# Order of the up and down units in a Strassen-Winograd MLP, and its sums by copies and adding DMAs

## The chip, the cores and the metric

The kernel runs on one core of one Trainium2 chip. A core has a matrix engine (TensorE, PE in the profile) that multiplies from SBUF into the accumulator memory PSUM, a vector engine (VectorE, DVE), an activation engine (ScalarE, ACT), GpSimd (POOL) and SyncE (SP), which here only issues DMAs. Each engine works through its own queue in order; semaphores make one wait for another. The metric is the device time of one execution in microseconds (us), lower is better. Three runs of the kernel before gave 1293.41 to 1295.04 us, median 1294.1 us.

## What is computed

A decoder trunk of two layers on one sequence of 512 tokens with 1024 channels, in float32. Cut to what matters here:

```python
for i in range(2):
    hn = rmsnorm(h, norm_mix_g[i])
    h = h + (even_mixer if i % 2 == 0 else odd_mixer)(hn, ...)
    hn = rmsnorm(h, norm_mlp_g[i])
    u = jnp.square(jax.nn.relu(hn @ w_mlp_up[i]))        # 1024 -> 4096
    h = h + u @ w_mlp_down[i]                            # 4096 -> 1024
    gate = jax.nn.sigmoid(rmsnorm(h, norm_ple_g[i]) @ w_ple_gate[i])
    h = h + (p[i] @ w_ple_proj[i]) * gate
return rmsnorm(h, final_norm_g)
```

The change concerns the squared-ReLU MLP, the two lines with `u`.

## The kernel before

Activations lie transposed: the eight tiles `h[0]` to `h[7]` hold 128 channels each by 512 tokens. To keep float32 accuracy, every operand is split into a high part (rounded to fp32r) and a low part (the rest), and each product is three matmuls, high by high, high by low, low by high (`mm3`, L140; the three matmuls are lines 141, 144 and 145). ACT makes a high part by a copy, DVE the low part by a subtraction.

**The MLP in quarters.** The 4096 hidden channels are worked in four quarters, `ch` = 0 to 3. A quarter has four *up units* `up(ch, c)`: each loads 1 MB of weights (`wload`, two buffers `raw`), splits them (L122, L128), and computes two hidden tiles of 128x512 in 48 matmuls of 512 columns. DVE applies ReLU and the norm's factor (L757), ACT squares (L758). The two tiles of a unit are one *pair*, and four tokens-by-channels quadrants of it, and three sums of them (`T1`, `T2`, `T4`, lines 763 to 767), are the seven slices of the tile `u`. ACT and DVE split it into `uh` (L769) and `ul` (L770), which are 7x256 columns each.

A quarter also has four *down units* `down(ch, c)`, one for every two output tiles `h[2c]`, `h[2c+1]`. They use the Strassen-Winograd form: a 2x2 block product with seven products in place of eight. DVE makes the four weight sums `s13` and `s24` (lines 794, 795, 796, 799), and `split` makes the high and low parts of `w13`, `w24`, `w11` and `w` (L808, L809). `w13`, `w24` and `w` have the tags `wh`/`wl` with three buffers, `w11` the tag `e` with five. Each of the seven products runs over the quarter's four pairs: 4 x 3 = 12 matmuls of 256 columns. They go to four PSUM banks. Banks 2 and 3 belong to `h` and are added there (L877, L878). Banks 0 and 1 belong to sums that several blocks share; they are gathered over the quarters in `sides[c][0]` and `sides[c][1]` (`total`: ACT copies in quarter 0, L838; DVE adds in quarters 1 and 2, L840), and put into `h` once, by `side_sums` (L921).

**The order of units** is written out by hand at the end of `mlp`:

```python
for c in range(4):
    up(0, c)
for ch in range(1, NCH):
    up(ch, 0)
    for c in range(4):
        down(ch - 1, c)
    for c in range(1, 4):
        up(ch, c)
```

So a quarter's down units come after the first up unit of the next quarter, and the hidden tiles `uh` and `ul` have five buffers each. After quarter 3's up units there is no such unit to come between; there, the first down unit takes the pairs in two passes, `ks` = (0, 1, 2) and then (3,) (L858). In quarter 3 two more things differ. The sums `s13` come from DRAM by two copies on SP's queue and an adding DMA on POOL's (`add_up`, lines 778 and 779). And `total` goes through `collect`: an ACT copy to a staging tile (L833) and an adding DMA on POOL's queue (L834) into `sides`. The staging is the tile `u`, or for `c` = 1 a spare buffer of `ul` called `stage`; another spare buffer, of `uh`, holds `b12` for the last, plain down unit `down_last` (L895).

Within an engine, a scheduler at compile time chooses the order of instructions from priorities (the order in which they are written) and its estimate of times; `order(later, earlier)` adds an edge that forbids the other order. The kernel uses it at the first down unit of quarter 3 for the weight splits against the ReLU and the sums of `u`.

## Time and profile before

| | |
|---|---|
| median of 3 runs | 1294.1 us |
| profiled execution | 1294.54 us |
| its span, first to last instruction | 1292.8 us |
| granted TensorE clock | 0.998 |
| ACT busy | 708.3 us, 55% |
| DMA, mean rate | 112 GB/s |
| HBM read, written | 131.92 MB, 6.37 MB |

The page gives the busy time of each engine, a table of 40 slices, and the costliest groups of instructions with the idle time ahead of them. Besides the page there are views of the trace: who waited for whom, windows with the busy time of each engine, and the timeline, which lists instructions by start time (us from the span's start), duration, engine, line, operation, tiles written and read, and in brackets the idle time of that engine just before, with what ended it. A matmul's duration overlaps the next one's, so that the pace of PE is read from the starts.

### The profile page before, as it was taken

How to read it: one execution, taken by the hardware profiler on the slowest of the kernel's cores; microseconds unless marked ns; L12 is line 12 of the kernel's file. 1: busy time of each engine (PE TensorE's matmuls, PEld its weight loads, DVE VectorE, ACT ScalarE, POOL GpSimd, SP SyncE). 2: the span in 40 equal slices, each digit the busy share in tenths (PEclk: the TensorE clock that was granted, in tenths of full speed). 3: DMA queues.
4: the chain of work that ended last, by engine and by line, in shares of the span. 5: the costliest groups of instructions: out<-in, count | busy, mean ns of one | idle time of the engine just before them, and what ended most of it. 6: DMA issues, size and time to landing. Idle time of an engine off the chain costs nothing.

```text
span 1292.8 us, 19230 instructions
## 1 busy us (share of the span) xinstructions
PE 1273.7 (99%) x7488; PEld 1121.4 (87%) x7488; DVE 1003.9 (78%) x1665; ACT 708.3 (55%) x1146; POOL 214.1 (17%) x184
## 2 busy tenths in 40 slices
PE   9999999999999999999999999999999999999996
PEld 7988887888988989989889888788899898898986
DVE  7788898688848869678767777887785885986976
ACT  5767868555535344356456666765553443534544
POOL 2343433500000000001024333222000000000201
PEclk9999999999999999999999999999999999999999
DMA  6421523222232322648332222212223223254751
GB/s 209 146 82 50 163 74 115 90 98 98 98 103 93 119 103 76 192 110 222 134 130 83 82 90 80 68 58 90 106 98 108 88 98 126 71 158 136 174 177 66
DMA packets 33995, 144.25 MB, mean 112 GB/s; under 512 B 3888, under 2 KB 4624, under 8 KB 21232
## 3 DMA queue, kind: packets, MB, share of 16 engines
q1 hardware_dynamic: 29680, 135.16, 30.7%
q0 software_dynamic: 4224, 7.87, 3.5%
q8 instruction: 59, 0.97, 0.3%
q14 instruction: 32, 0.26, 0.1%
HBM read 131.92 MB, written 6.37 MB: 107 GB/s over the span
## 4 chain that ended last, share of the span: by engine, by line
PE 81%; DVE 10%; ACT 5%; issue 2%; DMA 2%; SPq 0%; POOL 0%; DVEq 0%; ACTq 0%
PE mm L141 11%; PE mm L144 11%; PE mm L145 10%; PE sc L144 5%; PE sc L145 5%; PE sc L141 5%; PE pv L144 4%; PE pv L145 4%; PE pv L141 4%; PE tp L145 4%; PE tp L144 4%; PE tp L141 4%; PE pv L574 3%; PE tp L553 2%; PE tp L895 2%
## 5 line engine op out<-in xcount | busy, mean ns | idle before, releaser
L122 ACT ACTIVATE wh<-raw 128x1024 fp32r<-128x1024 f32 (+1 forms) x156 | 160.6, 1034 | 141.0 <-PE mm L144 52.9
L126 POOL TENSOR_TENSOR wl<-raw,wh 128x512 fp32r<-128x512 f32 (+1 forms) x132 | 179.7, 1383 | 299.1 <-ACT wh L122 295.4
L141 PE MATMUL mm<-hi,wh 128*128 128x512 f32 x472 | 186.3, 395 | 0.4 <-DVE tmp L490 0.4
L145 PE MATMUL mm<-hi,wl 128*128 128x512 f32 x472 | 184.7, 391 | 0.0
L144 PE MATMUL mm<-lo,wh 128*128 128x512 f32 x472 | 184.5, 391 | 0.0
L128 DVE TENSOR_TENSOR wl<-raw,wh 128x1024 fp32r<-128x1024 f32 x90 | 109.6, 1223 | 38.2 <-ACT wh L122 34.1
L145 PEld LDWEIGHTS mm<-hi,wl 128*128 128x128 f32 x472 | 88.6, 188 | 19.9 <-POOL wl L126 0.4
L141 PEld LDWEIGHTS mm<-hi,wh 128*128 128x128 f32 x472 | 88.7, 188 | 17.2 <-DVE tmp L490 0.8
L144 PEld LDWEIGHTS mm<-lo,wh 128*128 128x128 f32 x472 | 88.7, 188 | 15.6
L779 POOL DMA_DIRECT2D s<-in_w_down_dram x4 | 4.5, 1122 | 581.6 <-DMA s<-in_w_down_dram 315.8
L808 ACT ACTIVATE wh<-s 128x1024 fp32r<-128x1024 f32 x58 | 61.1, 1053 | 54.8 <-DVE s L795 14.7
L547 ACT ACTIVATE e<-e,mn 128x128 f32<-128x128 f32 (+3 forms) x96 | 53.8, 561 | 62.2 <-DVE mn L544 61.8
L770 DVE TENSOR_TENSOR ul<-u,uh 128x1792 fp32r<-128x1792 f32 x32 | 64.8, 2024 | 29.5 <-ACT uh L769 29.4
L809 DVE TENSOR_TENSOR wl<-s,wh 128x1024 fp32r<-128x1024 f32 x58 | 70.9, 1222 | 16.9 <-ACT wh L808 16.6
L769 ACT ACTIVATE uh<-u 128x1792 fp32r<-128x1792 f32 x32 | 54.5, 1702 | 45.7 <-DVE u L767 45.7
L758 ACT ACTIVATE u<-u 128x512 f32<-128x512 f32 x64 | 39.7, 626 | 68.1 <-DVE u L757 67.9
L141 PE MATMUL sc<-hi,wh 128*128 128x512 f32 x184 | 72.3, 393 | 0.4 <-ACT hi L187 0.4
L144 PE MATMUL sc<-lo,wh 128*128 128x512 f32 x184 | 72.1, 392 | 0.4 <-DVE lo L188 0.3
L145 PE MATMUL sc<-hi,wl 128*128 128x512 f32 x184 | 72.0, 391 | 0.0
L141 PE MATMUL mm<-wh,hi 128*128 128x256 f32 (+1 forms) x216 | 63.1, 292 | 0.0
L145 PE MATMUL mm<-wh,lo 128*128 128x256 f32 (+1 forms) x216 | 63.0, 292 | 0.0
L144 PE MATMUL mm<-wl,hi 128*128 128x256 f32 (+1 forms) x216 | 62.8, 291 | 0.0
(304 smaller groups left out, 3874.3 us busy)
## 6 DMA issues: line engine op xcount, KB each, us to landing
raw<-in_w_up_dram SPq DMA_DIRECT2D x32, 1024.0 KB, 4.9
raw<-in_w_down_dram SPq DMA_DIRECT2D x32, 1024.0 KB, 4.9
raw<-in_w_in_dram SPq DMA_DIRECT2D x23, 1024.0 KB, 4.9
raw<-in_w_gate_dram SPq DMA_DIRECT2D x8, 1024.0 KB, 4.9
bias<-urow SPq DMA_DIRECT2D x24, 256.0 KB, 3.9
raw<-in_w_outa_dram SPq DMA_DIRECT2D x8, 768.0 KB, 4.1
pj<-pjd SPq DMA_DIRECT2D x16, 256.0 KB, 4.9
h<-in_xT_dram SPq DMA_DIRECT2D x8, 256.0 KB, 6.5
```

Source lines behind the costliest of these rows:

```text
L122: act = nc.scalar.activation(hi, src, AF.Copy)
L126: nc.gpsimd.tensor_tensor(lo[:, kx], src[:, kx], hi[:, kx].bitcast(F32), op=ALU.subtract)
L128: last_low[:] = [nc.vector.tensor_tensor(lo, src, hi.bitcast(F32), op=ALU.subtract).ins]
L141: mm = nc.tensor.matmul(acc, lh, rh, start=start, stop=False)
L144: nc.tensor.matmul(acc, lh, rl, start=False, stop=False)
L145: return mm.ins, nc.tensor.matmul(acc, ll, rh, start=False, stop=stop).ins
L547: nc.scalar.activation(e[:, 0:n], e[:, 0:n], AF.Exp, scale=-1.0, bias=mn, accum_out=s)
L758: chain.append(nc.scalar.activation(ui, ui, AF.Square, scale=0.5).ins)
L769: nc.scalar.activation(uh, u, AF.Copy)
L770: part = nc.vector.tensor_tensor(ul, u, uh.bitcast(F32), op=ALU.subtract)
L808: high[:] = [nc.scalar.activation(hi, src, AF.Copy).ins]
L809: low[:] = [nc.vector.tensor_tensor(lo, src, hi.bitcast(F32), op=ALU.subtract).ins]
```

## The change

The matmuls stay as many as they were. The diff does five things.

- **Order.** In every quarter all four up units come first, then its four down units. The first down unit of each quarter, not of the last alone, takes the pairs in two passes, and the edges that `order` adds there hold in each quarter.
- **Buffers.** `uh` and `ul` have four buffers in place of five. `b12` has tiles of its own for each `c`, and `stage` is a tile of its own, written only as `s13` of `down(3, 1)`.
- **Side sums.** `total` in quarters 1 and 2 goes through `collect` as in quarter 3: an ACT copy, then an adding DMA on POOL's queue. In quarter 0 the ACT copies stay.
- **State sums.** In quarters 0 to 2 the additions to `h` go through `collect` too (with the sign -1 for the second). In quarter 3 they stay on DVE.
- **Staging.** `collect` takes its staging from the tag `e` (five buffers).

Besides, the zeroing of the left part of `diag` (the second operand of the scan at L619) goes from DVE at the start to POOL, behind the first mixer's other memsets.

```diff
-    nc.vector.memset(diag[:, 0:S - P], 0.0)
...
+        if keep:
+            nc.gpsimd.memset(diag[:, 0:S - P], 0.0)
...
+            uh, ul = (fpool.tile([P, 7, HW], F32R, tag=t, name=nm(t), bufs=4) for t in ("uh", "ul"))
             u = fpool.tile([P, 7, HW], F32, tag="u", name=nm("u"), bufs=1)
             if ch == NCH - 1:
-                if c == 0:
-                    b12.append([fpool.tile([P, HW], F32R, tag=t, name=nm(t), bufs=1) for t in ("b12h", "b12l")])
-                else:
-                    if c == 1:
-                        spare.append(fpool.tile([P, 7, HW], F32R, tag="uh", name=nm("spare"), bufs=5))
-                        stages.append(fpool.tile([P, 7 * HW], F32, tag="ul", name=nm("stage"), bufs=5))
-                        add_up(stages[0][:, 0:2 * S].rearrange("p (s c) -> p s c", s=2), w_down[layer, 4 * ch + 1])
-                    b12.append((spare[0][:, 2 * c - 2], spare[0][:, 2 * c - 1]))
-            uh = fpool.tile([P, 7, HW], F32R, tag="uh", name=nm("uh"), bufs=5)
-            ul = fpool.tile([P, 7, HW], F32R, tag="ul", name=nm("ul"), bufs=5)
+                b12.append([fpool.tile([P, HW], F32R, tag=f"{t}{c}", name=nm(t), bufs=1) for t in ("b12h", "b12l")])
+                if c == 1:
+                    stages.append(fpool.tile([P, 2, S], F32, tag="stage", name=nm("stage"), bufs=1))
+                    add_up(stages[0], w_down[layer, 4 * ch + 1])
...
-            if last and c:
+            if c and (last or c == 1):
                 order(sum2, hidden[ch, 3][2] if c == 1 else lows[-1])
...
-            if last:
-                stage = [stages[0] if c == 1 else fpool.tile([P, 7 * HW], F32, tag="u", name=nm("u"), bufs=1), 0]
-
             def collect(dst, src, sign=1.0):
-                t = stage[0][:, stage[1]:stage[1] + src.shape[-1]]
-                stage[1] += src.shape[-1]
+                t = t2k("e")[:, 0:src.shape[-1]]
                 nc.scalar.activation(t, src, AF.Copy, scale=sign)
                 nc.gpsimd.dma_start(dst, t, accum_op=ALU.add)
...
-                elif not last:
-                    nc.vector.tensor_tensor(sides[c][x], sides[c][x], banks[bank], op=ALU.add)
                 else:
                     collect(sides[c][x], banks[bank])
...
-            if last and c == 0:
+            if c == 0:
                 order(low[0], hidden[ch, 3][3])
             lows.append(low[0])
             w11 = split(rv[:, A11:A11 + 1])
-            if last and c == 1:
+            if c == 1:
                 order(low[0], low13)
-            if last and c == 0:
+            if c == 0:
                 lows.clear()
...
-            for ks in ((0, 1, 2), (3,)) if last and c == 0 else (range(4),):
+            for ks in ((0, 1, 2), (3,)) if c == 0 else (range(4),):
...
-                    if last and c == 0:
+                    if c == 0:
                         order(high[0], hidden[ch, 3][4])
                         order(low[0], hidden[ch, 3][5])
...
-            nc.vector.tensor_tensor(h[2 * c], h[2 * c], banks[2], op=ALU.add)
-            nc.vector.tensor_tensor(h[2 * c + 1][:, 0:HW], h[2 * c + 1][:, 0:HW], banks[3][:, 0:HW], op=ALU.subtract)
+            if last:
+                nc.vector.tensor_tensor(h[2 * c], h[2 * c], banks[2], op=ALU.add)
+                nc.vector.tensor_tensor(h[2 * c + 1][:, 0:HW], h[2 * c + 1][:, 0:HW], banks[3][:, 0:HW], op=ALU.subtract)
+            else:
+                collect(h[2 * c], banks[2])
+                collect(h[2 * c + 1][:, 0:HW], banks[3][:, 0:HW], -1.0)
...
+        for ch in range(NCH - 1):
+            for c in range(4):
+                up(ch, c)
+            for c in range(4):
+                down(ch, c)
         for c in range(4):
-            up(0, c)
-        for ch in range(1, NCH):
-            up(ch, 0)
-            for c in range(4):
-                down(ch - 1, c)
-            for c in range(1, 4):
-                up(ch, c)
+            up(NCH - 1, c)
         side_sums(3)
```

More of the change, by code (lines that the diff above doesn't have):

```diff
@@ L733, in mlp @@
         sides = [[fpool.tile([P, S], F32, tag=f"side{x}{c}", name=nm("side"), bufs=1) for x in range(2)] for c in range(4)]
-        hidden, spare, stages, b12, low, lows, high = {}, [], [], [], [], [], []
+        hidden, stages, b12, low, lows, high = {}, [], [], [], [], []
         def up(ch, c):
@@ L786, in down @@
             if last and c == 1:
-                s13 = stages[0][:, 0:2 * S].rearrange("p (s c) -> p s c", s=2)
+                s13 = stages[0]
             else:
```

## The prediction, made before the changed kernel had run

> **What bounds the kernel now.** I read the page's head first, then the list of what the tensor engine waits for, then a table of windows around the stretches that the change reorders, and last the timeline of three engines at one seam.
>
> ```profile
> span 1292.8 us, 19230 instructions
> PE 1273.7 (99%) x7488; PEld 1121.4 (87%) x7488; DVE 1003.9 (78%) x1665; ACT 708.3 (55%) x1146; POOL 214.1 (17%) x184
> ```
>
> TensorE (PE) is busy for all but 1292.8 - 1273.7 = 19.1 us. The change alters the order of its matmuls, not their number: 7 products, 4 pairs and 3 matmuls a down unit before and after. So a gain can only come out of these 19.1 us, or out of matmuls that are issued late without showing as idle. How much of that lies in the MLP stage (274 to 610 us, and the same again in the second layer)?
>
> ```profile
> PE sc L145 <- DVE wl L809: 1.1, 1, 1.1
> PE mm L144 <- DVE ul L770: 0.9, 2, 0.4
> ```
>
> Of the twelve kinds of wait that PE shows, these two are the MLP's. Three waits, 2.0 us in all. The table of windows says where (columns after the window: length, then busy time and count of PE, weight loads, DVE, ACT, POOL, then clock, DMA share and rate):
>
> ```profile
> 409.70:449.70 40.00, 40.00 (x338) 40.00 (x337) 32.98 (x43) 15.93 (x16) 0.00 (x0) 1.00 0.30 106
> 565.90:598.30 32.40, 30.84 (x254) 30.14 (x253) 28.81 (x46) 19.76 (x26) 6.76 (x8) 1.00 0.64 158
> 1191.50:1222.70 31.20, 30.72 (x254) 30.21 (x254) 27.72 (x44) 19.76 (x26) 6.11 (x7) 1.00 0.67 163
> ```
>
> The first row is the down part of the second quarter: PE has no idle time at all, although DVE is at 33.0 of 40.0 us. 4 x 84 = 336 matmuls in 40.0 us are 0.119 us each. The other two rows are the down units of the last quarter in the two layers. Only there does a down unit follow its own fourth up unit directly, and only there does PE wait. That is exactly the seam which the change makes at three more places in each layer. So the kernel before holds two samples of its price.
>
> **The seam, second layer.**
>
> ```profile
> 1191.55 0.28 PE L141 MATMUL mm<-uh,wh 128*128 128x256 f32 x1
> ...
> 1199.21 0.28 PE L141 MATMUL mm<-uh,wh 128*128 128x256 f32 x1
> 1199.93 0.39 PE L144 MATMUL mm<-ul,wh 128*128 128x256 f32 x1 [0.44 <-DVE ul L770]
> ...
> 1202.76 0.28 PE L144 MATMUL tp<-ul,wh 128*128 128x256 f32 x1
> 1203.07 0.39 PE L145 MATMUL tp<-uh,wl 128*128 128x256 f32 x1
> ```
>
> The first down unit begins at 1191.55. Its first pass takes pairs 0 to 2: 63 x 0.119 = 7.5 us. The second pass, pair 3, needs the fourth unit's `ul`. Its second matmul starts 0.72 us after the first where 0.12 is the pace: **0.60 us** lost. At 1203.07, in the next unit's first product, the low half of its weights is late: 0.31 - 0.12 = **0.19 us**. (Gaps under 0.06 us are left out of the price; the first quarter has some too, without such a seam.) Together 0.79 us.
>
> ```profile
> 571.47 0.28 PE L144 MATMUL sc<-ul,wh 128*128 128x256 f32 x1
> 572.83 0.38 PE L145 MATMUL sc<-uh,wl 128*128 128x256 f32 x1 [1.08 <-DVE wl L809]
> ...
> 574.83 0.28 PE L141 MATMUL mm<-uh,wh 128*128 128x256 f32 x1
> 575.55 0.39 PE L144 MATMUL mm<-ul,wh 128*128 128x256 f32 x1 [0.44 <-DVE ul L770]
> ```
>
> In the first layer the same 0.60 us, and 1.36 - 0.12 = **1.24 us** before it, for the weights of the last two products. The cause lies some 16 us earlier, in DVE's queue:
>
> ```profile
> 549.89 0.69 DVE L796 TENSOR_TENSOR s<-s,raw 128x512 f32<-128x512 f32 x1 [2.90 <-issue]
> 1174.28 0.69 DVE L796 TENSOR_TENSOR s<-s,raw 128x512 f32<-128x512 f32 x1 [1.59 <-DMA raw<-in_w_down_dram]
> ```
>
> The weight sum of the coming down unit stands in DVE's queue and holds everything behind it until its weights have landed: 2.90 us in one layer, 1.59 in the other. The difference, 1.31 us, is about the 1.24 that PE pays. In both cases the landing shared the DMA engines with the copies and sums from DRAM that only the last quarter makes.
>
> **The change part by part.**
>
> *Order of units.* Removed: the one up unit (10.9 us of PE) that lay between the fourth up unit and the down units of quarters 0 to 2. Added: two passes in the first down unit, as in the last quarter. What covered the chain from accumulator to `ul` is now the 7.5 us pass. Six new seams. I start from 0.79 us each and correct by rows:
>
> ```profile
> 1192.68 0.43 DVE L762 TENSOR_TENSOR spare<-u,spare 128x256 fp32r<-128x256 f32 x1
> 1193.02 0.68 DVE L757 SCALAR_TENSOR_TENSOR u<-pv,rstd 128x512 f32<-128x512 f32 x1
> ...
> 1197.85 2.03 DVE L770 TENSOR_TENSOR ul<-u,uh 128x1792 fp32r<-128x1792 f32 x1 [0.69 <-ACT uh L769]
> ...
> 1201.79 1.23 DVE L809 TENSOR_TENSOR wl<-stage,wh 128x1024 fp32r<-128x1024 f32 x1 [0.59 <-ACT wh L808]
> 1202.93 0.68 DVE L877 TENSOR_TENSOR h<-h,sc 128x512 f32<-128x512 f32 x1
> ...
> 1203.86 1.22 DVE L809 TENSOR_TENSOR wl<-s,wh 128x1024 fp32r<-128x1024 f32 x1
> ```
>
> - L762 is made in the last quarter only. In the chain it stands ahead of the second L757, 1193.02 - 1192.68 = **-0.34 us**.
> - Against that, quarters 0 to 2 make two more weight sums a unit on DVE (L794, L795, 0.69 us each), but without the landing delay of 1.59 to 2.90 us, since no copies from DRAM run beside it. These two nearly cancel in the second layer's sample. I take 0; bounds -0.26 (what is then left of the 0.60) and +1.24 (the first layer's lateness).
> - The order of products differs: in quarters 0 to 2 the first unit's `w13` is read by the first and the third product of a pass, in the last by the first and second. Its buffer, which the next unit's `w13` needs, is free one product later, 3 x 0.119 = **+0.36 us**. The 0.19 grows by that.
>
> ```profile
> 1200.70 1.06 ACT L808 ACTIVATE wh<-stage 128x1024 fp32r<-128x1024 f32 x1 [2.88 <-PE mm L144]
> 1201.66 1.07 ACT L833 ACTIVATE u<-mm 128x512 f32<-128x512 f32 x2
> 1202.62 1.06 ACT L808 ACTIVATE wh<-s 128x1024 fp32r<-128x1024 f32 x1
> ```
>
> - The next unit's `w24` is now wanted by its second product, not its third. Counted on the second layer's clock: unit start 1202.40, plus 0.55 (0.19 + 0.36), plus 12 x 0.119 for one product and 0.24 to the third matmul = 1204.62. Its low half: ACT 1202.62 to 1203.68, and without L877 ahead of it DVE to about 1204.97: **+0.35 us**. On ACT two copies went ahead of that split; with the h copies four would. Bounds: 0 (split first) and +1.3 (two more copies of 0.4 to 0.6 us ahead).
>
> So 0.79 - 0.34 + 0.36 + 0.35 = 1.16 us for a seam.
>
> *Sums by copies and adding DMAs.* Per down unit of quarters 1 and 2 DVE loses two side adds (L840) and two h adds (L877, L878); quarter 0 loses the h adds only. PE had no idle time there, so DVE's relief is worth **0**. ACT gains copies of about 0.55 us (L833 above); in the 40 us window ACT had 15.9 busy, so 16 x 0.55 = 8.8 more has room. The adding DMAs are issued on POOL, idle there (0.00 in the window). The staging is the `e` tag with its 5 buffers, and these the units' `w11` halves use too:
>
> ```profile
> L834 POOL DMA_DIRECT2D side<-u x8: 878/1201/1552, 578.2 to 1220.5; - x8
> DMA to landing us min/median/max: 3.3/4.9/6.0
> 428.33 0.62 ACT L808 ACTIVATE e<-raw 128x512 fp32r<-128x512 f32 x1
> 434.67 0.69 DVE L809 TENSOR_TENSOR e<-raw,e 128x512 fp32r<-128x512 f32 x1
> ```
>
> The two `w11` halves made at 428.33 and 434.67 are those of the unit that starts at 439.7 and are read until its fourth product ends at 445.4: 17.1 + 10.7 = 27.8 buffer-us a unit. Four copies hold a buffer for 0.6 + 4.9 us each, 22.0. Together 49.8 of the 5 x 10.0 that there are. It just fits, since `w11` can be made later. At the seam of quarters 1 and 2 the next unit's `w11` low half may have to wait until the first side copy has landed: copy by about 2 us into the second pass, landed at 7 to 8, DVE 0.69, wanted at 2.5 + 4.3 + 0.24 plus the seam's own 0.5 = 7.5. Bounds 0 and 1.2; I take **+0.2 us** for four of the six seams.
>
> By the Trainium skill, "SBUF — State Buffer", section "SBUF: two separate sides", a DMA issued by GpSimd can starve, since its descriptors are written through a port pair that some VectorE instructions lock. The rows agree in kind: the issue (L834) took 878 to 1552 ns. Its text has 620 ns alone against 3100 beside such an operation; as an estimate by that page, 2.5 us more for each of the adds. The sum does without it, and what it would do is a rival below.
>
> *Fewer buffers for `uh`/`ul`* (4 for 5). The next quarter's first up unit can write `uh` only after the last down unit has read it, but it does so after its own 10.9 us of matmuls: **0**. If that cover went, the next seam would be late; it is four units away.
>
> *The last quarter.* `stage` and `b12` have buffers of their own, so the copies and the sum from DRAM for unit 1 no longer wait for a `ul` buffer, and can be out of the way of the landing at 549.89. That would give back the first layer's lateness: **-1.24 us**; bounds 0 and -2.6 (all that both last seams lose: 1.84 + 0.79).
>
> *The memset.*
>
> ```profile
> 0.89 0.38 DVE L194 MEMSET diag<- 128x384 f32 x1 [0.89 <-PEq L1147]
> 25.43 5.58 POOL L126 TENSOR_TENSOR wl<-raw,wh 128x512 fp32r<-128x512 f32 x4 [21.26 <-ACT wh L122]
> ```
>
> 0.38 us go from DVE, which waits for the first loads anyway; on POOL it falls into 21.26 us of idle time: **0**.
>
> **Sum.** Quarter 0: 2 x 1.16 = 2.3. Quarters 1 and 2: 4 x 1.36 = 5.4. Last seam -1.24. Together +6.5 us. The profiled execution took 1294.54 us (1.7 around its span), so 1301.0; it lies 0.44 above the median of the three runs, 1294.1, and against that I forecast **1300.6**.
>
> **Rivals.**
>
> 1. *The seams are covered.* The chain from the last accumulator to `ul` needs, with nothing between, about 0.69 + 0.63 + 0.69 + 2 x 0.42 + 1.71 + 2.03 = 6.6 us and some 0.5 of hand-overs: under the 7.5 of the pass. If DVE comes to the seam without lateness and the splits are placed between, the six seams cost 0 to 0.6 us each and the last gives up to 1.2 back: 1293 to 1296.5. For it: no landing delay. Against it: both samples show 0.60. Chance 0.25.
> 2. *Faster.* All six seams are covered and both last seams lose their waits too: 1294.1 - 2.6 = 1291.5, and a few small gaps more make 1291. It can hardly go lower, since the waits in the list end there. Chance 0.10.
> 3. *The `e` buffers throttle the units.* With a hold of 0.6 + 6.0 us (the slowest landing) the need is 27.8 + 26.4 = 54.2 of 50 buffer-us, a unit of 10.8 us instead of 10.0, and 16 units in quarters 1 and 2 of both layers lose 13 us beside the 6.5: about 1314. It decides from a landing above 4.95 us, and the rows have a median of 4.9. Against it: DVE and ACT can make `w11` later, and a bank is wanted again only two units on. The rule of the Trainium skill above would work here, and L834's 1552 ns agrees with it as far as it goes. Chance 0.15.
>
> **How the numbers follow.** The forecast, six seams partly exposed and +2.7 to +13 us in all, has 0.50. This kernel's measurement can tell about 0.2%, 2.6 us, from no change. Faster by more: 0.10 (rival 2). Within it: 0.25 (rival 1). Slower: 0.50 + 0.15 = 0.65. The range goes from 1291.8, which takes in nearly all of rival 1 and some of rival 2, to 1310, where six seams with the first layer's lateness end (6 x (1.16 + 1.24) + 0.8 = 15.2 on 1294.1) and below which part of rival 3 lies; about 0.2 is left out.
>
> **What would show it.** Right: in the profile after, the last matmul of each fourth up unit is followed 7.5 us later by a PE wait for `ul` L770, six new ones, and about 12 us after the seam by one for `wl` L809; the windows of the down parts grow from 40.0 to 41 or 42 us, those of the up parts stay at 43.5. DVE's busy time falls by about 49 us (of each layer, 8 units lose 2 x 0.69 + 0.69 + 0.42 and 4 lose 1.11) without effect. Wrong: no PE wait at the seams (rival 1); or waits spread over all units of quarters 1 and 2, with ACT or DVE waiting for adding DMAs (rival 3). A different count of matmuls, or another pace than 0.119 us, would overturn the whole argument.

## The result and the profile after

The changed kernel took **1302.38 us** (median of 4 runs, 1301.29 to 1302.88) against 1293.76 us (1293.3 to 1295.04) for the kernel before, run beside it: a ratio of 1.0066, with a 95% interval of 1.0055 to 1.0078. It is slower by about 8.6 us. The profiled execution's span is 8.2 us longer (1301.0 against 1292.8).

The head of the page, for the kernel after:

```profile
span 1301.0 us, 19540 instructions
PE 1277.3 (98%) x7488; PEld 1121.2 (86%) x7488; DVE 963.4 (74%) x1584; ACT 744.9 (57%) x1226; POOL 283.6 (22%) x265
```

The matmuls are as many as before, 7488. DVE lost 40.5 us of work and ACT gained 36.6; neither engine is the bottleneck, PE is still busy for 98% of the span. PE's idle time grew by 4.6 us (19.1 to 23.7), and its busy time by 3.6 with the same matmuls: part of a wait counts as busy, as the last section shows. The list of PE's waits, kernel after (total us, times, longest):

```profile
PE tp L145 <- DVE wl L805: 3.1, 6, 0.5
PE sc L145 <- DVE wl L805: 2.2, 2, 1.1
PE mm L144 <- DVE ul L766: 0.9, 2, 0.4
```

The first row is new: six waits, one for each new seam, all for the low half of a weight block. The second had one entry before and has two. The third is as before: the last quarter's two seams and no others.

The windows of the down parts, kernel after (length, busy time and count of PE, weight loads, DVE, ACT, POOL, then clock, DMA share, GB/s):

```profile
399.70:440.60 40.90, 40.37 (x337) 40.09 (x336) 26.61 (x30) 23.75 (x32) 12.04 (x14) 1.00 0.80 180
568.60:612.80 44.20, 42.51 (x326) 40.41 (x325) 39.82 (x64) 26.60 (x37) 8.91 (x10) 1.00 0.71 177
1197.90:1242.20 44.30, 42.50 (x326) 40.39 (x325) 39.51 (x64) 26.56 (x37) 8.87 (x10) 1.00 0.72 177
```

In the second quarter DVE's work fell from 33.0 to 26.6 us, ACT's rose from 15.9 to 23.8, POOL's from nothing to 12.0, and the DMA engines' share from 0.30 to 0.80. The part is 1.0 us longer (40.97 us in the table below, 40.00 before).

For all kernels below I measured each down part from the start of its first matmul to the start of the first matmul behind it (us; quarters 0, 1, 2 and the last, of layer 0 and then of layer 1):

| kernel | layer 0 | layer 1 | six seams | two last |
|---|---|---|---|---|
| before | 40.32, 40.00, 40.00; 43.69 | 40.32, 40.00, 39.99; 42.38 | 240.63 | 86.07 |
| after | 41.37, 40.97, 40.87; 44.17 | 41.39, 41.09, 40.97; 44.31 | +6.03 | +2.41 |
| e4, order alone | 41.93, 40.43, 40.42; 42.19 | 41.92, 40.44, 40.44; 41.99 | +4.95 | -1.89 |
| e5, sums alone | 40.32, 41.28, 40.78; 47.14 | 40.31, 40.46, 41.11; 46.31 | +3.63 | +7.38 |
| e12, side sums moved | 41.37, 40.86, 40.87; 41.57 | 41.38, 40.86, 40.87; 41.57 | +5.58 | -2.93 |
| e6, before with two edges | 40.31, 40.00, 40.00; 41.57 | 40.32, 40.00, 40.00; 41.57 | +0.00 | -2.93 |

The kernel after: 6.03 + 2.41 = 8.4 us, which accounts for the 8.2 by which its span grew. Each row is one profiled execution, and that of the kernel after is the longest of its four. In the profiles of e1 and e10, whose medians agree with the change, the two last parts are together 1.3 and 2.2 us shorter, so a difference of 2 us there is not yet an effect. So there are two questions: what makes a new seam cost 1.0 us, and why the two last seams became slower where I had expected them to gain.

**A new seam.** The timeline of PE, then of ACT and DVE, at new seams of the kernel after (quarters 2 and 1):

```profile
494.70 0.28 PE L144 MATMUL tp<-ul,wh 128*128 128x256 f32 x1
495.51 0.39 PE L145 MATMUL tp<-uh,wl 128*128 128x256 f32 x1 [0.53 <-DVE wl L805]
495.74 0.28 PE L141 MATMUL tp<-uh,wh 128*128 128x256 f32 x1
```

```profile
404.69 2.03 DVE L766 TENSOR_TENSOR ul<-u,uh 128x1792 fp32r<-128x1792 f32 x1 [0.69 <-ACT uh L765]
...
408.13 0.60 ACT L825 ACTIVATE e<-mm 128x512 f32<-128x512 f32 x1 [3.48 <-PE mm L145]
408.63 1.05 ACT L804 ACTIVATE wh<-s 128x1024 fp32r<-128x1024 f32 x1
...
409.71 1.23 DVE L805 TENSOR_TENSOR wl<-s,wh 128x1024 fp32r<-128x1024 f32 x1 [1.67 <-ACT wh L804]
```

At 494.70 the next matmul comes 0.81 us later where 0.12 is the pace, 0.69 lost; the one behind it follows after 0.23, another 0.11. This is the first product of the second unit. The second block tells why its weights are late: the part began at 399.66, `ul` was ready at 406.72, which is 7.06 us in and so in time for the second pass at 7.5. The split of the second unit's `w13` on ACT (408.63) waits for a copy of a sum (408.13), and that for a matmul; DVE then waits 1.67 us for ACT.

**The last seam.** PE in layer 0, and DVE's queue some 30 us before it:

```profile
574.65 0.28 PE L144 MATMUL sc<-ul,wh 128*128 128x256 f32 x1
576.01 0.39 PE L145 MATMUL sc<-uh,wl 128*128 128x256 f32 x1 [1.08 <-DVE wl L805]
...
578.73 0.39 PE L144 MATMUL mm<-ul,wh 128*128 128x256 f32 x1 [0.44 <-DVE ul L766]
```

```profile
533.36 0.89 DVE L915 TENSOR_TENSOR side<-side,side 128x256 f32<-128x256 f32 x2 [8.77 <-DMA side<-e]
...
553.09 0.69 DVE L792 TENSOR_TENSOR s<-s,raw 128x512 f32<-128x512 f32 x1 [0.29 <-issue]
553.70 0.42 DVE L761 SCALAR_TENSOR_TENSOR u<-u 128x256 f32<-128x256 f32 x1
...
574.74 1.22 DVE L805 TENSOR_TENSOR wl<-raw,wh 128x1024 fp32r<-128x1024 f32 x1
576.65 2.03 DVE L766 TENSOR_TENSOR ul<-u,uh 128x1792 fp32r<-128x1792 f32 x1 [0.69 <-ACT uh L765]
```

The 1.24 us that layer 0 lost before are lost again, and layer 1 now loses them too. The weight sum that used to wait 2.90 us for its weights (L796 before, L792 now) waits 0.29. That is no gain yet, because DVE itself comes to it late: the first of the side sums of quarter 3 (L915) stands at the head of DVE's queue for 8.77 us, waiting for an adding DMA that the change has put into the path of its operand. In the kernel before, the same sum ran without a wait:

```profile
530.54 0.88 DVE L921 TENSOR_TENSOR side<-side,side 128x256 f32<-128x256 f32 x2
```

The list of DVE's waits in the kernel after says that both layers pay it:

```profile
DVE side L915 <- DMA side<-e: 17.4, 2, 8.8
```

My theory after reading this (**theory A**): a new seam costs 0.7 to 0.9 us through the second unit's `w13`, and the last seams lose because the head of DVE's queue waits for the side DMAs, which starts the quarter's chains late. Rivals: the loss at the last seam is the work of the sums wherever it stands; or the adding DMAs take too many `e` buffers.

### The profile page after: what moved, and what is told of

The parts are those of the page before. It is cut to its first block, busy times and chain, and to the rows that moved or that the text cites. A ratio compares the mean times of both kernels' runs of the same rounds, so it can differ in the third digit from the quotient of the medians.

```text
span 1301.0 us, 19540 instructions
## 1 busy us (share of the span) xinstructions
PE 1277.3 (98%) x7488; PEld 1121.2 (86%) x7488; DVE 963.4 (74%) x1584; ACT 744.9 (57%) x1226; POOL 283.6 (22%) x265
## 4 chain that ended last, share of the span: by engine, by line
PE 74%; DVE 13%; ACT 6%; issue 3%; DMA 3%; SPq 0%; POOL 0%; DVEq 0%; ACTq 0%; POOLq 0%
PE mm L144 10%; PE mm L141 10%; PE mm L145 10%; PE sc L144 4%; PE sc L145 4%; PE tp L145 4%; PE sc L141 4%; PE tp L141 4%; PE tp L144 4%; PE pv L145 3%; PE pv L141 3%; PE pv L144 3%; PE pv L575 3%; PE tp L554 2%; PE tp L889 2%
## 5 line engine op out<-in xcount | busy, mean ns | idle before, releaser
L144 PE MATMUL mm<-lo,wh 128*128 128x512 f32 x472 | 184.6, 391 | 0.0
L145 PEld LDWEIGHTS mm<-hi,wl 128*128 128x128 f32 x472 | 88.6, 188 | 19.9 <-POOL wl L126 0.4
L144 PEld LDWEIGHTS mm<-lo,wh 128*128 128x128 f32 x472 | 88.7, 188 | 15.6
L826 POOL DMA_DIRECT2D side<-e x44 | 39.8, 979 | 269.4 <-ACT e L825 269.2
L826 POOL DMA_DIRECT2D h<-e x48 | 43.6, 976 | 221.8 <-DVE wl L805 160.2
L144 PE MATMUL sc<-lo,wh 128*128 128x512 f32 x184 | 72.0, 391 | 0.6 <-DVE lo L188 0.6
```

The source lines that it names most:

```text
L144: nc.tensor.matmul(acc, lh, rl, start=False, stop=False)
L145: return mm.ins, nc.tensor.matmul(acc, ll, rh, start=False, stop=stop).ins
L826: nc.gpsimd.dma_start(dst, t, accum_op=ALU.add)
```

## The experiments

Every kernel here computes all of the reference. Ratios are to the kernel before, with 95% intervals.

### The last seam: e1, e12, e8, e9, e10

**e1.** The call of the side sums written behind the first down unit.

```diff
-        side_sums(3)
         for c in range(3):
             down(NCH - 1, c)
+            if c == 0:
+                side_sums(3)
```

> The changed kernel with one call moved: side_sums(3) is written behind down(3, 0) and no longer ahead of it. Theory A (the last seam got worse because these sums stand in DVE's queue and wait 8.77 and 8.6 us for the adding DMAs of the quarter before, and all of quarter 3's chains start some 3.4 us late): no DVE wait for a side DMA at the start of quarter 3, the 1.24 us wait for the fourth weight split gone in both layers, the last down part (252 products and down_last) down from 44.2 to about 42.0 us in each layer, the whole some 4 us below the changed kernel, about 1298. Theory B (the last seam is late by its own extra work, the copies of b12, whatever these sums do): the 1.24 us stay and the time stays at 1302. The six new seams cost 6.0 us under both.

Measured 1302.21 us, 1.0068 (1.0053 to 1.0083), the same as the change. But the timeline of DVE shows that nothing had moved:

```profile
532.63 0.88 DVE L915 TENSOR_TENSOR side<-side,side 128x256 f32<-128x256 f32 x2 [7.63 <-DMA side<-e]
```

The compile-time scheduler put the sums where it believed that their operands would be ready. The run decides nothing between the theories.

**e12.** The same call, written behind the first up unit of quarter 3 and held there by edges: `hidden[ch, c][2]` is the instruction that makes `ul`.

```diff
         for c in range(4):
             up(NCH - 1, c)
-        side_sums(3)
+            if c == 0:
+                side_sums(3, [hidden[NCH - 1, 0][2]])
```

> The kernel after, with the call of the side sums of quarter 3 put behind up(3,0), so that they stand in VectorE's queue behind ul(3,0), among the up units, by when their adding DMAs (which landed at about 533 us) have long landed. Theory A (the last seams are slow because the head of VectorE's queue waits 8.8 us in each layer for the adding DMAs of the side sums, which starts quarter 3's chains some 3.4 us late and issues the first weight blocks of the last seam late): no wait of VectorE for side sums, the 1.24 us waits of TensorE in the first unit of the last down part gone in both layers, these parts from 44.2 and 44.3 us to 41.6 to 43; the six other seams stay at 41.0 to 41.4 us; total 1298 (1296.5 to 1300). Rival B (it is the work itself and not its place: the 3.4 us of sums, wherever they stand, hold up the chains): the last parts stay at 44 us, total 1302, the same as the change. Rival C (later weight sums come late in turn, as where the sums were tied behind ul of (3,3)): the first unit of the last part recovers, the second loses as much, total 1302 to 1305.

Measured **1297.46 us** (7 runs), 1.0030 (1.0019 to 1.0042); the interval lies wholly below that of the change. DVE, and the window of the last down part of layer 0:

```profile
541.29 2.03 DVE L766 TENSOR_TENSOR ul<-u,uh 128x1792 fp32r<-128x1792 f32 x1 [1.83 <-ACT uh L765]
543.24 0.42 DVE L915 TENSOR_TENSOR h<-h,side 128x256 f32<-128x256 f32 x1
...
571.41 1.22 DVE L805 TENSOR_TENSOR wl<-raw,wh 128x1024 fp32r<-128x1024 f32 x1
```

```profile
568.30:609.90 41.60, 41.59 (x326) 40.28 (x325) 36.92 (x61) 25.54 (x35) 7.84 (x9) 1.00 0.72 184
```

The sums now run between other work, with no wait. The last block of weights is split at 571.41, 3.1 us into the part (which begins at 568.29); in the kernel after it is split at 574.74, 6.2 us into a part that begins at 568.56. So the wait had set DVE back by 3 us all the way to the seam. The last parts fall from 44.17 and 44.31 to 41.57 each, and the six other seams stay as they were: theory A. The work of the sums is the same in both kernels, so it was their place. Over the runs, too, the last part of layer 0 shrinks with the wait at its side sums: 8.77 us and 44.17 in the kernel after, 7.63 and 43.10 in e1, 6.57 and 42.70 in e10, no wait and 41.57 here.

With DVE no longer held up, the weight sum waits for its weights again, 1.39 us here and 1.49 in layer 1, and the last parts lose nothing by it:

```profile
550.90 0.43 DVE L763 SCALAR_TENSOR_TENSOR u<-u 128x256 f32<-128x256 f32 x1
552.72 0.69 DVE L792 TENSOR_TENSOR s<-s,raw 128x512 f32<-128x512 f32 x1 [1.39 <-DMA raw<-in_w_down_dram]
```

Here it stands behind the last sum of `u` (L763), so that ACT makes `uh` during the wait. In the kernel before, two of these sums stood behind it (lines 765 and 767, at 550.50 and 551.44) and waited with it.

**e8.** The sums placed later still: behind `ul` of the fourth unit, at the seam itself.

```diff
-        side_sums(3)
         for c in range(3):
             down(NCH - 1, c)
+            if c == 0:
+                side_sums(3, [hidden[NCH - 1, 3][2]])
```

> The changed kernel with side_sums(3) held behind the ul of quarter 3's last up unit on DVE by order edges. In e1 the call stood later in the text, but the trace shows the sums still at the old place in DVE's queue, with the same wait of 7.6 us for side DMAs in the first layer. Theory A (that wait is what makes quarter 3 late): no DVE wait for a side DMA ahead of quarter 3, the 1.24 us wait of PE gone in both layers, the last down parts from 44.2 us to 42 or a little more for the sums themselves (8 x 0.42 us on DVE after the seam), in all 3 to 4.5 us below the changed kernel, about 1298.5. Theory B (b12 and the splits make it): the 1.24 us stay, 1302.

Measured 1304.98 us, 1.0092 (1.0077 to 1.0108), with a wide spread: 1303.27 to 1306.89 in four runs, of which the profile is the shortest. The first unit of the last part recovers, from 12.64 and 12.79 us to 10.19 and 10.78. The second one loses as much, from 10.27 in both to 12.51 and 12.60:

```profile
580.33 0.39 PE L141 MATMUL pv<-uh,wh 128*128 128x256 f32 x1 [1.26 <-ACT wh L804]
...
581.58 0.39 PE L145 MATMUL tp<-uh,wl 128*128 128x256 f32 x1 [0.75 <-DVE wl L805]
```

The eight sums, at least 0.33 us each, now stand among and in front of the second unit's weight sums and splits. The same work, three places: in front of the up units it costs by its wait, at the seam by its length, among the up units nothing.

**e9.** Why do the side DMAs land so late? In POOL's queue of the kernel after an adding DMA of weights stands among them and waits for its two sources:

```profile
519.84 1.08 POOL L775 DMA_DIRECT2D s<-in_w_down_dram  x1 [4.19 <-DMA s<-in_w_down_dram]
520.56 1.29 POOL L826 DMA_DIRECT2D h<-e  x1
521.13 2.50 POOL L826 DMA_DIRECT2D side<-e  x2
```

So I tied it behind the latest of `collect`'s DMAs, which `added[0]` holds.

```diff
-            nc.gpsimd.dma_start(s13, sv[:, A22:A11 + 1:2], accum_op=ALU.add)
+            add = nc.gpsimd.dma_start(s13, sv[:, A22:A11 + 1:2], accum_op=ALU.add).ins
+            order(add, added[0])
...
-                nc.gpsimd.dma_start(dst, t, accum_op=ALU.add)
+                added[:] = [nc.gpsimd.dma_start(dst, t, accum_op=ALU.add).ins]
```

> The changed kernel with the adding DMA of quarter 3's weight sum (L775) held behind the last adding DMA of down(2, 3) on POOL's queue. Theory A (that DMA stands in POOL's queue 4.2 us for its copies from DRAM; the adding DMAs behind it start late, their e buffers stay taken, an ACT copy waits 4.6 us for a buffer, and with it the side sums on DVE): the ACT waits for adding DMAs at that place and DVE's wait for the side DMA fall from 8.8 us to 4 or less, the last seam gets better by 0.5 to 2 us a layer, 1299 to 1301. Against it stands that the weight sum then lands later: if s24 or w13 of down(3, 0) waits for it, the gain is lost. Theory B (the five e buffers alone hold the copies up): the waits stay as they are.

Measured 1322.68 us, 1.0223 (1.0206 to 1.0240), a failure that taught something else. DVE's wait for the side DMAs did fall, from 17.4 us in both layers to 6.6:

```profile
527.67 0.88 DVE L916 TENSOR_TENSOR side<-side,side 128x256 f32<-128x256 f32 x2 [3.57 <-DMA side<-e]
```

And the first units of the last parts did gain (12.64 to 10.73 and 12.79 to 11.78). But POOL's wait of 4.19 us had not delayed the issue of the DMA that DVE waits for. In the kernel after, ACT's copy for it ended at 521.90, POOL issued it at 522.19, and it landed 11.1 us later. In e9 it was issued at 521.69, as soon behind its copy, and landed after 5.9 us. From 514 to 533 us the DMA engines' share is 1.08 and 1.06, so they had no room in either kernel. What differs is the order: in the kernel after, the large DMA of the weight sum and the two that had queued up behind it were issued just ahead of the last side DMA, and in e9 the weight sum's came behind it.

The edge also holds back the weight sum of `down(3, 2)`, and PE waits for it for more than 6 us in each layer (timeline of PE, then windows behind it):

```profile
595.79 0.58 PE L141 MATMUL mm<-uh,wh 128*128 128x256 f32 x1 [6.55 <-ACT wh L805]
```

```profile
596.00:602.00 6.00, 5.74 (x26) 5.45 (x27) 5.93 (x12) 2.06 (x3) 0.00 (x0) 0.51 0.12 19
602.00:608.00 6.00, 6.00 (x53) 6.00 (x52) 4.25 (x8) 5.29 (x8) 2.60 (x3) 1.00 0.67 208
```

The column before the DMA share is the granted clock: 0.51 for the 6 us behind the wait, in which PE does 26 matmuls where 53 fit. The wait is paid for once as idle time and again, by some 3 us, as a slow clock.

**e10.** Six `e` buffers instead of five.

```diff
-    T_BUFS = {"e": 5, "tmp": 1, "tmp2": 3}
+    T_BUFS = {"e": 6, "tmp": 1, "tmp2": 3}
```

> The changed kernel with six buffers for the tag e in place of five. Theory A (the buffers throttle): ACT's waits for adding DMAs (10.3 us for h and 9.6 us for sides over the run) fall by half or more, DVE's wait in front of quarter 3 (17.4 us for both layers) gets shorter, and the time falls by 1 to 3 us, mostly at the last seam. Theory B (the landing of the adding DMAs, with the DMA engines at 0.80 busy, sets these waits and not the number of buffers): no change, 1302. The seams of quarters 1 and 2 stay at 0.87 us under both.

Measured 1302.53 us, 1.0071 (1.0056 to 1.0086): no change against the change. From the waits of ACT, first in the kernel after, then with six buffers:

```profile
ACT e L825 <- DMA h<-e: 10.3, 3, 4.6
ACT e L825 <- DMA side<-e: 9.6, 5, 3.1
```

```profile
ACT e L825 <- DMA h<-e: 2.4, 2, 1.3
```

ACT's waits for buffers go from 19.9 to 2.4 us, and the median does not notice. DVE's wait at L915 falls only from 17.4 to 14.8 us in both layers together. The profiled execution, the shortest of the four, has last parts of 42.70 and 43.62 us, and the two intervals leave room for a gain of 2 to 3 us. More than that of the 8.6 us was not in these buffers.

### A new seam: e2, e3, e7

**e2.** In the first unit of quarters 0 to 2 the products stand in the last quarter's order, so that `w13` is read by the first two and its buffer is free one product earlier.

```diff
-                if last:
+                if last or c == 0:
                     product(1, 0, w13, 1, T3, True, False, ks)
...
-                if not last:
+                if not last and c:
```

> The changed kernel with the products of the first down unit of quarters 0 to 2 in the order of quarter 3, so that w13 is read by the first two products of each pass and not by the first and third. Theory A (the next unit's w13 is late because its buffer comes free with the last reading in the second pass): each of the six waits of 0.68 us falls by 3 x 0.119 = 0.36 us to about 0.33, the whole by 2.1 us to about 1300. Theory B (the split is late on ACT behind the copy of a side sum): the waits stay at 0.6 to 0.7 and the time at 1302.

Measured 1300.85 us, 1.0062 (1.0046 to 1.0079). The 0.69 at each new seam falls to 0.17 to 0.19, and the second unit from 10.85 us to 10.25 in three of the four of quarters 1 and 2. ACT, at the seam of quarter 1 (the part begins at 399.09):

```profile
407.44 1.06 ACT L804 ACTIVATE wh<-s 128x1024 fp32r<-128x1024 f32 x1 [3.35 <-PE mm L144]
```

The split of `w13` now waits for PE's last reading of the buffer (mm L144) and starts 8.35 us into the part, where it started 8.97 us in. So the late release of the buffer sets a large part of the wait, as predicted. It is not the whole difference: the copies of the sums, one of which stood ahead of this split, now come behind it. But two third units lose 0.65 and 0.81 us, waiting for the low half of `w11` (in an `e` buffer). DVE makes it behind three weight sums and a split, and the first of these sums had to wait 1.60 and 1.67 us for its weights:

```profile
420.88 0.69 DVE L790 TENSOR_TENSOR s<-raw 128x512 f32<-128x512 f32 x1 [1.60 <-DMA raw<-in_w_down_dram]
...
424.57 0.39 PE L145 MATMUL mm<-uh,e 128*128 128x256 f32 x1 [0.49 <-DVE e L805]
```

Of the six seams' 6.03 us, 4.57 remain, and the gain in the median, 1.5 us, is within what the two intervals leave open.

**e3.** A buffer of its own for the first unit's `w13`.

```diff
-            def split(src):
+            def split(src, own=None):
...
-                    hi, lo = (wpool.tile([P, 2, 4, P], F32R, tag=t, name=nm(t), bufs=3) for t in ("wh", "wl"))
+                    hi, lo = (fpool.tile([P, 2, 4, P], F32R, tag="w13" + t, name=nm(t), bufs=1) if own else
+                              wpool.tile([P, 2, 4, P], F32R, tag=t, name=nm(t), bufs=3) for t in ("wh", "wl"))
...
-            w13 = split(s13)
+            w13 = split(s13, c == 0)
```

> The changed kernel with buffers of its own for the w13 of each quarter's first down unit, so that the next unit's w13 has to wait for no reading. Theory A (buffer): all waits for wl at the start of the second down unit are gone, 0.87 us less at each of the new seams and 0.30 at the last ones, 5 to 6 us in all, about 1296.5. Theory B (ACT's or DVE's queue): a wait of 0.3 us or more stays at that place, or turns up one or two products later.

Measured 1309.49 us, 1.0125 (1.0110 to 1.0141). At the seams theory A holds: four of the six down parts (quarters 0 and 1) are at 40.4 to 40.5 us, the last ones at 41.21 and 41.99. The loss is elsewhere, at the end of the two parts of quarter 2 (44.00 and 46.39 us). With a buffer free, the scheduler put the split of quarter 3's `w13` early into ACT's queue, where it waits for an adding DMA, ahead of the splits of the up weights that PE wants (ACT, PE, then windows):

```profile
524.27 1.06 ACT L805 ACTIVATE wh<-s 128x1024 fp32r<-128x1024 f32 x1 [6.69 <-DMA s<-in_w_down_dram]
```

```profile
526.32 0.67 PE L141 MATMUL mm<-hi,wh 128*128 128x512 f32 x1 [3.62 <-ACT wh L122]
```

```profile
526.30:530.00 3.70, 3.33 (x7) 2.19 (x8) 2.64 (x3) 3.10 (x5) 2.01 (x3) 0.54 0.52 82
530.00:534.00 4.00, 4.00 (x19) 3.29 (x18) 1.99 (x3) 0.14 (x1) 0.56 (x1) 1.00 0.87 243
```

Again the wait is followed by a granted clock of about half, here after 3.6 us of idle PE; the up units behind it took 45.66 and 46.84 us in place of 43.5.

**e7.** e1 and e3 together.

> The changed kernel with side_sums(3) written behind down(3, 0) and with buffers of its own for the w13 of each quarter's first down unit, both at once. If the two repairs act on separate places, the gains add: 5 to 6 us from the buffers and 4 us from the sums, about 1293, the same as the kernel before within 0.2%. If they share a cause (ACT or DVE late for both), the sum of the gains is smaller and the time stays above 1295.

Measured 1308.85 us, 1.0118 (1.0101 to 1.0135): e3 again, with waits of 4.6 and 4.2 us at the same place. Since e1's edit moves nothing, it tells nothing more.

### The two halves of the change: e4, e5, e11

**e4.** The new order, with the sums on DVE.

```diff
+                elif not last:
+                    nc.vector.tensor_tensor(sides[c][x], sides[c][x], banks[bank], op=ALU.add)
                 else:
                     collect(sides[c][x], banks[bank])
...
-            if last:
+            if True:
                 nc.vector.tensor_tensor(h[2 * c], h[2 * c], banks[2], op=ALU.add)
```

> The new order of units alone: side and state sums of quarters 0 to 2 are DVE adds as before, all else as in the changed kernel. Theory A (the seams come from the order, the worsening of the last seam from the adding DMAs): the six new seams stay at about 0.9 to 1.0 us each, the last down parts go back to about 43 us, in all some 2.4 us below the changed kernel, about 1300. Theory B (the adding DMAs and their copies on ACT make the seams too): the seams fall to 0.5 us or less and the time to about 1296. Theory C (DVE, with 2.5 us more a unit, comes late to the seams): they grow to 1.5 us or more, the time stays at 1302 or above.

Measured 1297.08 us (6 runs), 1.0032 (1.0021 to 1.0044). The order alone makes the last seams faster, by 1.89 us, and the six new seams cost 4.95: 1.6 in quarter 0, but 0.43 in quarters 1 and 2. PE at the seam of quarter 1, where the part begins at 399.40:

```profile
409.84 0.28 PE L144 MATMUL tp<-ul,wh 128*128 128x256 f32 x1
410.18 0.39 PE L141 MATMUL pv<-uh,wh 128*128 128x256 f32 x1
410.40 0.27 PE L144 MATMUL pv<-ul,wh 128*128 128x256 f32 x1
410.52 0.36 PE L145 MATMUL tp<-uh,wl 128*128 128x256 f32 x1
```

The matmul with the low half comes 11.12 us into the part; in the kernel after it came at 410.99, 11.33 us in. The 0.21 between them goes with the 0.60 us copy that stands ahead of the split on ACT there. The rest is PE's own order: here two matmuls of another product fill the wait.

**e5.** The old order, with the sums through `collect` and its staging in `e`.

```diff
-            if last:
-                stage = [stages[0] if c == 1 else fpool.tile([P, 7 * HW], F32, tag="u", name=nm("u"), bufs=1), 0]
...
-                t = stage[0][:, stage[1]:stage[1] + src.shape[-1]]
-                stage[1] += src.shape[-1]
+                t = t2k("e")[:, 0:src.shape[-1]]
...
-                elif not last:
-                    nc.vector.tensor_tensor(sides[c][x], sides[c][x], banks[bank], op=ALU.add)
                 else:
                     collect(sides[c][x], banks[bank])
...
+            if last:
                 nc.vector.tensor_tensor(h[2 * c], h[2 * c], banks[2], op=ALU.add)
...
+            else:
+                collect(h[2 * c], banks[2])
+                collect(h[2 * c + 1][:, 0:HW], banks[3][:, 0:HW], -1.0)
```

> The kernel before with one part of the change: side and state sums of quarters 0 to 2 by ACT copies into the e tag and adding DMAs. The order of the units is the old one. Theory A (the sums cost nothing where no seam is exposed, and harm only through DVE's wait in front of quarter 3): the down parts of quarters 0 to 2 stay at 40.0 to 40.3 us, DVE waits for a side DMA in front of the last quarter's up units, and the last down parts grow by 0.5 to 2 us each; in all 1 to 4 us above the kernel before, 1295 to 1298. Theory B (the five e buffers throttle the units): the down parts of quarters 1 and 2 grow by a microsecond or more each, in all 4 us or more.

Measured 1306.07 us, 1.0096 (1.0081 to 1.0111). The sums alone cost more than the whole change: 7.38 us at the last seams and 3.63 in quarters 1 and 2, there mostly in the third units, where PE waits for the low half of `w11`. DVE at the start of the side sums (L919 in this kernel):

```profile
544.63 0.89 DVE L919 TENSOR_TENSOR side<-side,side 128x256 f32<-128x256 f32 x2 [10.16 <-DMA side<-e]
```

In the old order only three up units lie between these sums and the last seam, in the new one all four. The same kind of wait, 10.16 us against 8.77, then leaves the last seams 7.38 us slower than before and not 2.41. That the fourth up unit in between hides the difference fits, but e5 differs in more than this distance and doesn't isolate it.

**e11.** e5 with the edges of e8 and e9.

> The kernel before with the copies and adding DMAs for the sums (as in e5) and with both edges: side_sums(3) behind the last ul on DVE, the weight sum's adding DMA behind the other adding DMAs on POOL. e5 lost 12 us: 3.6 in quarters 1 and 2 and some 7.4 at the last seams. Theory A (the last seams' loss is the wait of DVE in front of quarter 3 and POOL's queue): the last down parts fall from 47.1 and 46.3 us to 42 to 43.5, the down parts of quarters 1 and 2 stay 0.5 to 1.3 us too long, in all 1297 to 1299. Theory B (the adding DMAs slow everything by their landing time): 1303 or more.

Measured 1328.58 us, 1.0276 (1.0261 to 1.0292). The first units of the last parts gain (15.61 and 14.79 us to 11.78 and 11.93), and the weight sum of `down(3, 2)` is late by 5.8 and 5.4 us, with the slow clock behind it, as in e9. That the time came out above 1303 does not speak for theory B, since the edge on POOL made a wait of its own.

### The kernel before, without its late landing: e6

The prediction read the 1.24 us of the kernel before as a weight sum that stood in DVE's queue before its weights had landed. Two edges on the kernel before put that sum behind `ul` of unit (3, 1) on DVE, and the split of `w11` behind `uh` of it on ACT (`[6]` is the instruction that makes it).

```diff
+            if last and c == 0:
+                order(sum2, hidden[ch, 1][2])
...
+            if last and c == 0:
+                order(high[0], hidden[ch, 1][6])
```

> The kernel before with two more order edges at the last seam: the weight sum s24 of down(3, 0) goes behind the ul of unit 1 on DVE, and the high part of its w11 behind the uh of unit 1 on ACT, so that the wait for the landing of the weights (2.90 and 1.59 us on DVE, 4.18 and 2.83 us on ACT) holds up no chain. Theory A (the prediction's: the wait for the landing is what makes the first layer's seam 1.24 us worse than the second's): the 1.24 us are gone, the last down parts fall from 43.69 and 42.38 us to about 42, the whole by 1.5 to 2.5 us to about 1292. Theory B (the lateness comes from elsewhere in quarter 3, its b12 or the order of its splits): the 1.24 us stay or move.

Measured **1291.34 us** (10 runs), 0.9982 (0.9972 to 0.9991): a little faster than both kernels, and the fastest of all here. Both last parts are at 41.57 us; the window of layer 0:

```profile
565.30:606.90 41.60, 41.59 (x326) 40.28 (x325) 36.67 (x60) 24.99 (x34) 7.80 (x9) 1.00 0.72 180
```

The 1.24 and both 0.60 are gone; 0.17 and 0.10 remain in the second unit. So the 0.60 for `ul`, which I had taken for the base price of a seam, was no property of the seam either: it was lateness that came down the queues. Since both edges were set at once, DVE's share and ACT's are not told apart. e12 with the products of e2 was not tried.

## Why the prediction was right and where it was wrong

The forecast, 1300.6 us, was 1.8 us low, and its sign and kind were right: no step that frees DVE gains anything, and six new seams cost some microseconds. That it came so near is partly luck: the six seams were put 1.7 us too high and the two last ones 3.65 us too low, and the two errors offset each other in part. Of the signs that I named, the waits for the second unit's `wl` and down parts of 41 us came, and the six waits for `ul` did not. Step by step:

- **The bound held.** 7488 matmuls, a pace of 0.119 us in the down parts, and up units as long as before: between the parts of quarters 1 and 2 there are 43.5 us in both kernels.
- **Six new seams: +7.7 forecast, +6.03 measured.** The terms were not all the right ones. The `ul` wait did not come in quarters 1 and 2: the list shows two, those of the last quarter. I had left 0.26 of its 0.60; the bound -0.26, which leaves nothing, was the right end there. In quarter 0 a small one came, 0.17 us: `ul` is ready 8.0 us into the part (at 322.76, read at 322.82). There is no landing delay at these seams, and e6 shows that the 0.60 went when that delay held nothing up. The `w13` term, 0.19 + 0.36 = 0.55, measured 0.69, at the place given, 0.45 us into the second unit, and e2 shows that the later release is a large part of it, while the copies on ACT add 0.21 (e4). Two short pauses of about 0.10 us beside each wait, which I had left out as too small, make it about 0.9. The `w24` term of 0.35 did not come at all: the copies delayed `w13` instead. The 0.2 for the `e` buffers came in no seam of the kernel after.
- **Sums by copies and adding DMAs: 0 forecast; wrong.** This is the step that failed. Between e4 and the change, 1.0032 to 1.0066, the sums cost 0.34%, 4.4 us; by the down parts 1.1 us at the six seams and 4.3 at the last ones. I checked that ACT and POOL had room and that the buffers sufficed, but not who reads the sums. The last adding DMAs of quarter 2 feed the side sums, which come next in DVE's queue. An add on DVE hands its result on in its own queue; an adding DMA here lands 2.6 to 11.2 us after its issue (the last row counts those into `h` too):

```profile
L826 POOL DMA_DIRECT2D side<-e x44: 856/856/1952, 409.0 to 1229.3; - x44
...
DMA to landing us min/median/max: 2.6/5.2/11.2
```

- **The last seam: -1.24 forecast, +2.41 measured.** The gain was there, but not quite by the route that I gave. With the sums on DVE (e4) the seams gain 1.89, and with the side sums moved (e12) 2.93, all that my bound of -2.6 allowed and a little more. The copies for `stage` did get out of the way, and the weights take 4.9 us from their issue to the sum that reads them (548.24 to 553.09), where they took 8.9 (540.98 to 549.89). But they are issued later, so that the sum starts 15.5 us ahead of the last part and not earlier than before (16.0). DVE still waits for them where nothing else holds it up, 1.42 and 1.20 us in e4. What a landing wait costs depends on what stands behind it, as e6 and e12 show. In the kernel after, the side sums' wait of 8.8 us took up the gain and more.
- **DVE's relief: 49 us forecast, 40.5 measured**, worth 0 as said. Back to back, an add of 0.69 us takes only 0.61 of the queue (the rows at 553.09 and 553.70 above), and busy time counts the overlap once. I had added durations; with the distances between starts, 0.61 and 0.33, the same adds come to 42 us.
- **Fewer `uh`/`ul` buffers and the memset: 0.** No wait in the lists points to either.

**The rivals.** Rival 1 (covered seams) had the chain right: 6.6 + 0.5 = 7.1 us forecast, 7.06 measured in quarter 1, under the pass of 7.5. It was wrong in taking that for the whole seam. Rival 3 had its condition fulfilled, a median landing of 5.2 us above its 4.95, and ACT did wait 19.9 us for the adding DMAs; but e10 takes these waits away without a gain that four runs can resolve, so they were covered in the main, as its counter-argument said. Rival 2 had the last seams right, as e12 shows, and the six others wrong. By the Trainium skill, "SBUF — State Buffer", section "SBUF: two separate sides", a DMA issued by GpSimd takes about 620 ns alone and about 3100 ns beside a VectorE copy that keeps GpSimd from writing its descriptors. The trace has the issue of the side DMAs, 856 ns in the median and 1952 at most, and no run here tells what VectorE's instructions have to do with it.

**What stays open.** Why DVE is about a microsecond later at the seams of quarter 0 than at the others: the 0.21 and 0.17 us that the first units lose there are waits for a weight block's low half (ready at 317.39, read at 317.44) and for `ul`. And whether the side DMAs would land in time with the weight sum's DMA moved to where nothing waits for it: e9 moved it, but to a place that made another wait.

## What to carry to other kernels

When a sum moves from a compute engine to a DMA, look first at its reader: an in-order queue whose head waits for a landing passes the delay to everything behind it, here from 8.8 us of idle DVE to 1.24 us of PE 40 us later. Place such a reader where its operand has long landed and the next deadline is still far (among the up units, e12), neither as early as data flow allows nor at the deadline. The same holds for a wait for weights: it is free where another engine works on what comes next (e12), and costs where the queue behind it feeds that engine. And an edit that moves one instruction must be followed through the queue to every other place that it touches: e3, e9 and e11 lost more at another unit than they gained.

## What the runs showed of the hardware

- **Behind an idle TensorE the granted clock fell to half, here from 3.6 us on, and in e11 behind less.** Behind the wait of e3 (3.62 us) the granted clock was 0.54 for 3.7 us, behind that of e9 (6.55 us) 0.51 for 6 us; behind e5's longest wait at the seam (1.67 us) it stayed at 1.00. The Trainium skill, "TensorE: Matmul & The Clock Gate", section "What's actually happening", puts the idle window at about 3.4 us and the slow state at half the clock; these rows agree. Shorter waits close together can do it too, and there no idle time of that length was needed: in e11 PE was busy for 1.40 of 3.40 us around two waits of 1.25 and 0.75 us, and then ran at half the clock:

```profile
1223.70:1227.10 3.40, 3.40 (x18) 3.40 (x17) 2.47 (x3) 0.00 (x0) 0.00 (x0) 0.51 0.17 31
```

In e8 the same pair of waits left the clock at 1.00 in both layers. The waits of the change itself, 1.1 us at most, left it at 1.00 in both last parts.
- **A wait costs more than its bracket shows.** The wait of 0.53 us at 495.51 lost 0.69 from start to start, and 0.11 more at the next matmul. The bracket counts from the end of the matmul before, which lasts 0.28 us where the pace is 0.12, so the first 0.16 us of the delay count as busy.
